# Transposes of x in pairs between the k and v matmuls of a transformer block on one core

## The chip, the core and the metric

The kernel runs on one core of a Trainium2 chip. The metric is the device time of one execution in microseconds (us). The core has five engines that run side by side, each working through its own instructions in order: PE does matmuls and transposes into PSUM banks, DVE, ACT and POOL work on tiles, SP issues the loads and stores. An instruction that needs another engine's result waits for a semaphore, and all that stands behind it on its own engine waits too.

## The reference

One layer of an encoder block, in float32, on x of 1024 rows and 1024 columns:

```
h = RMSNorm(x)
[q | k | v | u] = h @ w_in                 # widths 512, 128, 128, 512
a = GQA(q, k, v)                           # 8 query heads, 2 kv heads, axial RoPE, bidirectional
p = (windowed_mean(u) - u) @ pool_w + pool_b, times pool_scale   # 4 groups
x = x + concat([a, p]) @ w_out
x = x + SwiGLU(RMSNorm(x))                 # inner width 2816
```

## The kernel before

x lies in SBUF as eight tiles of 128 rows, `qp[:, t, :]`. PE needs it transposed, so for each of the eight column blocks k PE transposes the block of every row tile of a group (L474, one transpose of 128x128 for each tile) into one PSUM bank. The bank is emptied in two instructions: ACT multiplies by the norm's gain and writes the high part (L464), then DVE writes what is left of the value as the low part (L466). The full-precision product is made of three matmuls on high and low parts, and this holds for every product of the kernel.

`kv_tile(t)` projects row tile t to k and v. For each k it issues three matmuls of 128x256 (L490) into one bank, and at the end ACT (L498, L502) and DVE (L504) empty that bank. While a tile is projected, the next group of rows is transposed. `weave(tiles, ts)` mixes the two on PE: `tiles` are projected, and `turn_x(ts)` is advanced from time to time, one k at each step. The groups are rows 0, 1, 2 to 3 and 4 to 7, so there are three weaves with transposes: tile 0 projected while tile 1 is transposed (one transpose for each k), tile 1 while tiles 2 and 3 are (two), tiles 2 and 3 while tiles 4 to 7 are (four). Then tiles 4 to 7 are projected with no transposes between.

The banks: even k takes a bank of pool b1 (four banks, shared with the accumulators of `kv_tile`), odd k one of pool b2 (two banks). A transpose that takes a used bank waits until DVE's L466 has read it.

Around this stand the sums of squares of x (L451 on ACT) with a chain of tiny DVE instructions that make 1/rms of each row (L362 to L373), and the splitting of weights of w_in, loaded as 128x1024 pieces, into high and low parts: the high part on whichever engine the planner finds (L340 on ACT, L344 on POOL), the low part in `combine` (L355), on DVE or POOL. After the projections `spread_r` (L669) uses diagonal matrices of 1/rms, made 128 columns at a time on ACT (L656) and DVE (L658).

The order on PE follows the code. What other engines do is added as jobs to a planner (`flow`), which keeps an estimated time for each engine and a rank for each job, and writes each engine's instructions down in the order in which it lets them start; where an operation may run on two engines it takes the one that it holds to be free sooner. So what PE does earlier or later in the code changes the order on ACT, DVE and POOL too.

Of the kernel before, what the change touches and what calls it, by code (L numbers as in the profile page):

```python
# [289 lines left out]
def block_kernel(  # L290
# [167 lines left out]
    def turn_x(ts):  # L458
        n = len(ts) * P
        c0 = ts[0] * P  # L460

        def evacuate(hi, lo, pt, k):
            yield act(n, 0.05)
            nc.scalar.activation(hi, pt[:, :n], AF.Copy, scale=g1[:, k:k + 1])  # L464
            yield dve(n)
            nc.vector.scalar_tensor_tensor(lo, pt[:, :n], g1[:, k:k + 1], hi.bitcast(F32), op0=ALU.mult, op1=ALU.subtract)  # L466

        for k in range(NK):
            flow.now = max([flow.now] + [x_at[t, k] for t in ts])
            wide = k % K["wide"] == K["wide"] - 1  # L470
            pt = bank2()[:, 0:512] if wide else bank()
            flow.tensor(0.107 * len(ts))
            for i, t in enumerate(ts):
                nc.tensor.transpose(pt[:, i * P:(i + 1) * P], qp[:, t, k * P:(k + 1) * P], ident)  # L474
            job = flow.add(evacuate(hT(0, k, c0, n), hT(1, k, c0, n), pt, k))
            flow.hold("b2" if wide else "b1", job)
            for t in ts:
                x_turned[t, k] = job
            yield
# [4 lines left out]
    def kv_tile(t):  # L484
        pk = bank()
        for k in range(NK):
            hi, lo, job = wkv[k]
            flow.tensor(0.354, job, x_turned[t, k])
            for i, (a, b) in enumerate(PASSES):
                nc.tensor.matmul(pk[:, :2 * KW], hT(a, k, t * P, P), (hi, lo)[b], start=(k == 0 and i == 0), stop=(k == NK - 1 and i == 2))  # L490
            if k < NK - 1:
                yield

        def evacuate():
            r = rx[:, t:t + 1]
            yield [rx_job[t]]
            yield act(KW, 0.1)
            nc.scalar.activation(qp[:, t, AW:AW + KW], pk[:, 0:KW], AF.Copy, scale=r)  # L498
            pv = pk[:, KW:2 * KW].rearrange("p (h d) -> p h d", d=HD)
            hi, lo = vv[:, t, :, 0, :], vv[:, t, :, 1, :]  # L500
            yield act(KW, 0.1)
            nc.scalar.activation(hi, pv, AF.Copy, scale=r)  # L502
            yield dve(KW)
            nc.vector.scalar_tensor_tensor(lo, pv, r, hi.bitcast(F32), op0=ALU.mult, op1=ALU.subtract)  # L504

        kv_job[t] = flow.add(evacuate())
        flow.hold("b1", kv_job[t])
        yield
# [424 lines left out]
    def weave(tiles, ts=None):  # L933
        turns = turn_x(ts) if ts else None
        for i, b in enumerate([b for g in [kv_tile(t) for t in tiles] for b in [g] * NK]):
            next(b, None)
            if turns and i % len(tiles) == 0:
                next(turns, None)

    units = [(t, kv) for t in range(NT) for kv in range(NKV)]  # L940
# [589 lines left out]
    for i, ts in enumerate(groups):  # L1530
        for j in range(0, len(ts), 2):
            stats_x(ts[j:j + 2])
        for w, when in enumerate(K["take"]):
            if when == i:
                take_w(w)
        if i == K["tables"]:
            tab_job = load_tables()
        if i > 0 and ts[0] >= 4 and not kf:
            kf.append(flow.add(k_finish(0, 4)))
        weave(ts, groups[i + 1] if i + 1 < len(groups) else None)  # L1540
# [172 lines left out]
```

## Time and profile before

| | |
|---|---|
| median of 3 runs | 1082.85 us (1082.71 to 1082.98) |
| the profiled execution | 1083.04 us |
| its span in the trace | 1081.0 us |
| PE busy | 1061.1 us, 98% of the span |
| DVE busy | 742.1 us |
| ACT busy | 513.6 us |
| POOL busy | 459.0 us |

The span runs from the first to the last instruction in the trace; 2.04 us of the profiled execution's own time lie outside it, and that execution took 0.19 us more than the median. Busy shares are over the whole span: the stretch that the change touches ends some 32 us after its start.

### The profile page before, as it was taken

How to read it: one execution, taken by the hardware profiler on the slowest of the kernel's cores; microseconds unless marked ns; L12 is line 12 of the kernel's file. 1: busy time of each engine (PE TensorE's matmuls, PEld its weight loads, DVE VectorE, ACT ScalarE, POOL GpSimd, SP SyncE). 2: the span in 40 equal slices, each digit the busy share in tenths (PEclk: the TensorE clock that was granted, in tenths of full speed). 3: DMA queues.
4: the chain of work that ended last, by engine and by line, in shares of the span. 5: the costliest groups of instructions: out<-in, count | busy, mean ns of one | idle time of the engine just before them, and what ended most of it. 6: DMA issues, size and time to landing. Idle time of an engine off the chain costs nothing.

```text
span 1081.0 us, 13923 instructions
## 1 busy us (share of the span) xinstructions
PE 1061.1 (98%) x5114; PEld 876.2 (81%) x5114; DVE 742.1 (69%) x1210; ACT 513.6 (48%) x912; POOL 459.0 (42%) x371
## 2 busy tenths in 40 slices
PE   7999999999999999999999999999999999999998
PEld 6887877878888888878878887888788878888787
DVE  7888678788776766784984479355954496448845
ACT  6614478666666654633343433434433443343340
POOL 3153444444223223463643555345534464445431
PEclk9999999999999999999999999999999999999999
DMA  7212110000000100221023102220212013110114
GB/s 260 69 40 79 39 59 30 10 21 10 20 21 11 30 21 30 59 98 39 19 68 109 39 1 78 78 79 1 78 59 76 23 33 104 59 40 20 40 58 156
DMA packets 42707, 58.47 MB, mean 54 GB/s; under 512 B 4240, under 2 KB 32784, under 8 KB 42640
## 3 DMA queue, kind: packets, MB, share of 16 engines
q1 hardware_dynamic: 42640, 57.59, 16.9%
q8 instruction: 40, 0.66, 0.2%
q14 instruction: 27, 0.22, 0.1%
HBM read 53.39 MB, written 4.19 MB: 53 GB/s over the span
## 4 chain that ended last, share of the span: by engine, by line
PE 79%; DVE 10%; issue 3%; POOL 3%; ACT 3%; DMA 1%; SPq 0%; POOLq 0%; ACTq 0%; DVEq 0%
PE b L1180 36%; PE b L912 8%; PE b L1498 8%; PE b L875 5%; PE b L832 5%; PE b L862 4%; PE b L688 4%; PE b L601 3%; DVE wk L355 3%; POOL wk L355 2%; PE b L1445 2%; DVE qp L1460 2%; PE b L490 2%; DVE ring L355 1%; DVE nm L841 1%
## 5 line engine op out<-in xcount | busy, mean ns | idle before, releaser
L1180 PE MATMUL b<-wk,ring 128*128 128x512 f32 x1872 | 426.8, 389 | 1.2 <-POOL ring L355 0.9
L1180 PEld LDWEIGHTS b<-wk,ring 128*128 128x128 f32 x1872 | 351.0, 188 | 75.6 <-POOL ring L355 1.8
L340 ACT ACTIVATE ring<-raw 128x512 fp32r<-128x512 f32 x130 | 81.5, 629 | 121.2 <-PE b L1180 59.9
L851 POOL TENSOR_SCALAR wk<-wk,rsm 128x1024 f32<-128x1024 f32 x64 | 75.0, 1180 | 132.9 <-PE b L862 40.7
L349 DVE TENSOR_TENSOR wk<-b,wk 128x512 fp32r<-128x512 f32 (+1 forms) x160 | 102.0, 659 | 42.5 <-ACT wk L340 42.1
L340 ACT ACTIVATE wk<-b 128x512 fp32r<-128x512 f32 (+1 forms) x160 | 90.4, 577 | 82.6 <-PE b L862 65.6
L355 POOL TENSOR_TENSOR ring<-raw,ring 128x512 fp32r<-128x512 f32 x49 | 63.3, 1292 | 149.5 <-ACT ring L340 136.0
L1498 PE MATMUL b<-raw,ring 128*128 128x512 f32 x480 | 113.4, 393 | 1.1 <-DVE qp L1460 1.1
L355 DVE TENSOR_TENSOR ring<-raw,ring 128x512 fp32r<-128x512 f32 x81 | 63.7, 789 | 72.2 <-ACT ring L340 71.7
L1498 PEld LDWEIGHTS b<-raw,ring 128*128 128x128 f32 x480 | 88.6, 188 | 24.3 <-DVE qp L1460 3.8
L1460 DVE TENSOR_TENSOR qp<-qp,b 128x512 f32<-128x512 f32 (+1 forms) x157 | 100.5, 673 | 9.0 <-PE b L1445 8.9
L912 PE MATMUL b<-wk 128*128 128x512 f32 x384 | 102.5, 397 | 0.0
L355 POOL TENSOR_TENSOR wk<-wk 128x512 fp32r<-128x512 f32 (+3 forms) x51 | 71.5, 1409 | 43.5 <-ACT wk L340 20.3
L832 PE MATMUL b<-kT,wk 128*128 128x512 f32 x256 | 89.4, 431 | 0.3 <-ACT wk L808 0.3
L875 PE MATMUL b<-wk,vv 128*128 128x512 f32 x256 | 82.7, 399 | 3.9 <-DVE wk L349 3.9
L841 DVE TENSOR_REDUCE nm<-b 128x1 f32<-128x1024 f32 x64 | 78.0, 1219 | 11.3 <-PE b L832 10.2
L1498 PE MATMUL b<-wk,ring 128*128 128x512 f32 x360 | 83.3, 389 | 0.0
L912 PEld LDWEIGHTS b<-wk 128*128 128x128 f32 x384 | 70.7, 188 | 14.9
L1498 PEld LDWEIGHTS b<-wk,ring 128*128 128x128 f32 x360 | 67.5, 188 | 14.2
L862 PEld LDWEIGHTS b<-ident,wk 128*128 128x128 f32 x512 | 63.6, 140 | 16.5
L862 PE MATMUL b<-ident,wk 128*128 128x128 f32 x512 | 76.4, 272 | 0.0
L843 ACT ACTIVATE wk<-b,nm 128x1024 f32<-128x1024 f32 x64 | 71.4, 1116 | 10.4 <-DVE nm L841 9.5
(144 smaller groups left out, 1445.1 us busy)
## 6 DMA issues: line engine op xcount, KB each, us to landing
raw<-in_w_gate_dram SPq DMA_DIRECT2D x22, 512.0 KB, 3.7
raw<-in_w_up_dram SPq DMA_DIRECT2D x22, 512.0 KB, 3.9
wk<-in_w_down_dram SPq DMA_DIRECT2D x20, 512.0 KB, 4.7
raw<-in_w_in_dram SPq DMA_DIRECT2D x10, 512.0 KB, 3.8
raw<-in_w_out_dram SPq DMA_DIRECT2D x8, 512.0 KB, 3.5
out_dram<-qp SPq DMA_DIRECT2D x15, 256.0 KB, 2.0
qp<-in_x_dram SPq DMA_DIRECT2D x7, 512.0 KB, 9.7
raw<-in_x_dram SPq DMA_DIRECT2D x14, 256.0 KB, 2.8
```

The source lines that it names most:

```text
L340: nc.scalar.activation(hi, src, AF.Copy)
L349: nc.vector.tensor_tensor(lo, src, hi.bitcast(F32), op=ALU.subtract)
L355: (nc.gpsimd if way[0] == "G" else nc.vector).tensor_tensor(dst, a, b, op=op)
L832: nc.tensor.matmul(s[:, c * 512:(c + 1) * 512], qT[t][0][:, h * P:(h + 1) * P], kT[:, kv, b, c * 512:(c + 1) * 512], start=(b == 0), stop= ...
L841: nc.vector.tensor_reduce(nm, s, axis=AX, op=ALU.max, negate=True)
L851: nc.gpsimd.tensor_scalar(pe, pe, rs, 1.0, op0=ALU.mult, op1=ALU.mult)
L862: nc.tensor.transpose(pt[:, j * P:(j + 1) * P], pe[:, c * P:(c + 1) * P], ident)
L875: nc.tensor.matmul(po[t, kv], vt, ps[:, b], start=(c == 0 and b == 0), stop=(c == NT - 1 and b == 1))
L912: nc.tensor.matmul(self.py, mix[self.t][a][:, k, :], wo[k][b][:, self.cs], start=(self.i == 0 and i == 0), stop=(self.i == NK - 1 and i == 2))
L1180: nc.tensor.matmul(bank_, w[0][:, a, i], x[:, b], start=(start and i == 0 and j == 0), stop=(stop and i == PARTS - 1 and j == 2), skip_gro ...
L1460: nc.vector.tensor_tensor(dst, dst, src, op=op)
L1498: nc.tensor.matmul(banks[t][0], x[:, a, t * P:(t + 1) * P], y[:, b], start=(own == name and i == 0 and j == 0), stop=(i == 1 and j == 2), ...
```

## The change

In `weave`, transposes are issued for one k after every k-step of the tiles together. Now they are issued for two k after every second such step:

```diff
         for i, b in enumerate([b for g in [kv_tile(t) for t in tiles] for b in [g] * NK]):
             next(b, None)
-            if turns and i % len(tiles) == 0:
+            if turns and i % (2 * len(tiles)) == 0:
+                next(turns, None)
                 next(turns, None)
```

On PE, in the third weave (tiles 2 and 3 projected, four transposes for each k), this is the order before from the first matmuls of tile 2 on. Numbers such as `b_356` name one bank tile; `b_349` and `b_415` are the accumulators of tiles 2 and 3.

```order
L490 MATMUL b_349<-wk 128x256 x3
L474 MATMUL b_356<-ident,qp 128x128 x4
L490 MATMUL b_349<-wk 128x256 x6
L474 MATMUL b_371<-ident,qp 128x128 x4
L490 MATMUL b_349<-wk 128x256 x6
L474 MATMUL b_392<-ident,qp 128x128 x4
L490 MATMUL b_349<-wk 128x256 x6
L474 MATMUL b_405<-ident,qp 128x128 x4
L490 MATMUL b_349<-wk 128x256 x3
L490 MATMUL b_415<-wk 128x256 x3
L474 MATMUL b_427<-ident,qp 128x128 x4
L490 MATMUL b_415<-wk 128x256 x6
```

And the same stretch with the change; accumulators are now `b_347` and `b_414`, and the transposes' banks in turn of k are `b_353`, `b_359`, `b_389`, `b_396`, `b_426`, `b_432`, `b_456`, `b_462`.

```order
L490 MATMUL b_347<-wk 128x256 x3
L474 MATMUL b_353<-ident,qp 128x128 x4
L474 MATMUL b_359<-ident,qp 128x128 x4
L490 MATMUL b_347<-wk 128x256 x12
L474 MATMUL b_389<-ident,qp 128x128 x4
L474 MATMUL b_396<-ident,qp 128x128 x4
L490 MATMUL b_347<-wk 128x256 x9
L490 MATMUL b_414<-wk 128x256 x3
L474 MATMUL b_426<-ident,qp 128x128 x4
L474 MATMUL b_432<-ident,qp 128x128 x4
L490 MATMUL b_414<-wk 128x256 x12
L474 MATMUL b_456<-ident,qp 128x128 x4
```

The transposes of every odd k have moved ahead of six matmuls (in the two weaves before, of three); the sixth of the eight, `b_442` before and `b_432` now, has 15 matmuls of its weave behind it before and 21 now.

On DVE, in the same weave, before (`b1` and `b2` are the pools of the banks, `raw` a loaded weight, L355 a weight's low part, L362 to L373 the chain for 1/rms):

```order
L466 SCALAR_TENSOR_TENSOR wk_116<-b2_340,pk_72,wk_108 128x256
L466 SCALAR_TENSOR_TENSOR wk_117<-b1_356,pk_72,wk_109 128x512
L355 TENSOR_TENSOR wk_175<-raw_172,wk_174 128x1024
L504 SCALAR_TENSOR_TENSOR vv_94<-b1_261,rx_121,vv_94 128x2x64
L362 TENSOR_SCALAR ms_387<-ssq1_122 128x2
L466 SCALAR_TENSOR_TENSOR wk_117<-b2_371,pk_72,wk_109 128x512
L364 TENSOR_SCALAR ra_388<-ms_387 128x2
L466 SCALAR_TENSOR_TENSOR wk_118<-b1_392,pk_72,wk_110 128x512
```

And with the change:

```order
L466 SCALAR_TENSOR_TENSOR wk_117<-b1_353,pk_72,wk_109 128x512
L371 SCALAR_TENSOR_TENSOR ra_274<-ra_274,ms_273 128x1
L355 TENSOR_TENSOR wk_175<-raw_172,wk_174 128x1024
L373 SCALAR_TENSOR_TENSOR rx_121<-ra_274,rx_121 128x1
L466 SCALAR_TENSOR_TENSOR wk_118<-b1_389,pk_72,wk_110 128x512
L362 TENSOR_SCALAR ms_384<-ssq1_122 128x2
L466 SCALAR_TENSOR_TENSOR wk_117<-b2_359,pk_72,wk_109 128x512
L504 SCALAR_TENSOR_TENSOR vv_94<-b1_261,rx_121,vv_94 128x2x64
L364 TENSOR_SCALAR ra_385<-ms_384 128x2
```

The 128x1024 weight split L355 still follows the first emptying (L466 of `b_353`), but two instructions of the 1/rms chain now lie around it; the emptyings of the second and third k have changed places, and with the emptying of tile 1's accumulator (L504 of `b_261`) they stand behind the split.

On ACT, at the end of the projections, before (`b_569` and `b_608` are the accumulators of tiles 6 and 7, L673 empties the first bank of `spread_r`):

```order
L656 ACTIVATE wk_651<-ident_73,rx_121 128x128 x4
L498 ACTIVATE qp_84<-b1_569,rx_121 128x128
L502 ACTIVATE vv_94<-b1_569,rx_121 128x2x64
L656 ACTIVATE wk_651<-ident_73,rx_121 128x128 x4
L498 ACTIVATE qp_84<-b1_608,rx_121 128x128
L673 ACTIVATE wk_672<-b1_673 128x512
```

And with the change (tile 7's accumulator is `b_611`):

```order
L498 ACTIVATE qp_84<-b1_569,rx_121 128x128
L656 ACTIVATE wk_655<-ident_73,rx_121 128x128 x4
L502 ACTIVATE vv_94<-b1_569,rx_121 128x2x64
L498 ACTIVATE qp_84<-b1_611,rx_121 128x128
L502 ACTIVATE vv_94<-b1_611,rx_121 128x2x64
L656 ACTIVATE wk_655<-ident_73,rx_121 128x128 x4
```

The second four diagonals now stand behind both instructions that empty tile 7's bank, and on DVE L658 for them stands behind that tile's L504. Beyond this stretch SP's order is the same in every row and the matmuls of the feed-forward part are too, except for the pool that some banks come from; of the weight splits with 128x1024 elements two that DVE did (one in the attention, the load of w_out) are done by POOL.

## Rows read from the trace of the kernel before

**Rows 1.** The page: busy time of each engine.

```profile
PE 1061.1 (98%) x5114; PEld 876.2 (81%) x5114; DVE 742.1 (69%) x1210; ACT 513.6 (48%) x912; POOL 459.0 (42%) x371
```

**Rows 2.** Windows; stretch, length, busy PE, PEld, DVE, ACT, POOL; granted clock, DMA share, GB/s.

```profile
10.66:15.50 4.84, 4.84 (x23) 4.84 (x24) 4.19 (x18) 1.90 (x6) 1.98 (x3) 1.00 1.03 420
15.50:31.80 16.30, 14.84 (x125) 14.28 (x125) 15.24 (x48) 12.78 (x28) 5.57 (x4) 1.00 0.61 176
...
200.00:1060.00 860.00, 856.48 (x4030) 705.40 (x4029) 572.59 (x844) 401.51 (x704) 379.56 (x291) 1.00 0.15 45
```

**Rows 3.** PE's waits by line and releaser: us in total, times, longest.

```profile
PE b L474 <- DMA qp<-in_x_dram: 5.0, 2, 4.3
PE b L875 <- DVE wk L349: 3.9, 7, 1.4
...
PE b L474 <- DVE wk L466: 1.5, 2, 1.3
...
PE b L601 <- POOL wk L355: 0.9, 1, 0.9
```

**Rows 4.** The chain of waits on PE: start, duration, what.

```profile
12.63 0.21 PE b L474
12.85 0.64 PE b L490 x3
...
15.96 0.12 PE b L474
...
30.46 0.44 PE b L474 x4
30.90 0.71 PE b L490 x6
...
32.05 11.88 PE b L490 x99
```

**Rows 5.** PE's timeline: start, duration, instruction, idle before it and the releaser.

```profile
19.37 0.41 PE L474 MATMUL b<-ident,qp 128*128 128x128 f32 x2 [0.18 <-DVE ra L369]
...
21.70 0.60 PE L474 MATMUL b<-ident,qp 128*128 128x128 f32 x4
...
29.09 0.66 PE L474 MATMUL b<-ident,qp 128*128 128x128 f32 x4 [1.28 <-DVE wk L466]
...
43.77 1.55 PE L688 MATMUL b<-wk 128*128 128x512 f32 x6
45.15 1.07 PE L669 MATMUL b<-wk 128*128 128x512 f32 x4
```

**Rows 6.** DVE's timeline in the third weave.

```profile
24.12 2.00 DVE L355 TENSOR_TENSOR wk<-raw,wk 128x1024 fp32r<-128x1024 f32 x1
26.05 0.34 DVE L504 SCALAR_TENSOR_TENSOR vv<-b,rx,vv 128x128 fp32r<-128x128 f32 x1
26.31 2.07 DVE L362 TENSOR_SCALAR ms<-ssq 128x2 f32<-128x2 f32 x1
28.30 0.74 DVE L466 SCALAR_TENSOR_TENSOR wk<-b,pk,wk 128x512 fp32r<-128x512 f32 x1
28.95 0.15 DVE L364 TENSOR_SCALAR ra<-ms 128x2 int32<-128x2 int32 x1
```

**Rows 7.** POOL's timeline in the third weave.

```profile
24.01 1.05 POOL L344 TENSOR_SCALAR wk<-raw 128x1024 fp32r<-128x1024 f32 x1 [3.26 <-DMA raw<-in_w_in_dram]
25.14 3.21 POOL L355 TENSOR_TENSOR wk<-raw,wk 128x1024 fp32r<-128x1024 f32 x1
```

**Rows 8.** ACT's timeline in the third weave: sum of squares, then one emptying.

```profile
23.30 1.06 ACT L451 ACTIVATE wk<-qp 128x1024 f32<-128x1024 f32 x1
...
24.59 0.70 ACT L464 ACTIVATE wk<-b,pk 128x512 fp32r<-128x512 f32 x1
```

**Rows 9.** Timeline of ACT and DVE before `spread_r`.

```profile
42.88 0.38 ACT L502 ACTIVATE vv<-b,rx 128x128 fp32r<-128x128 f32 x1
43.13 1.29 ACT L656 ACTIVATE wk<-ident,rx 128x128 fp32r<-128x128 f32 x4
...
43.63 1.18 DVE L658 SCALAR_TENSOR_TENSOR wk<-ident,rx,wk 128x128 fp32r<-128x128 f32 x4
```

**Rows 10.** Timeline in the attention: PE's waits and the DVE split ahead of the first.

```profile
157.55 1.23 DVE L355 TENSOR_TENSOR wk<-raw,wk 128x1024 fp32r<-128x1024 f32 x1
...
160.57 0.50 PE L875 MATMUL b<-wk,vv 128*128 128x512 f32 x1 [0.60 <-DVE wk L349]
...
180.49 0.50 PE L875 MATMUL b<-wk,vv 128*128 128x512 f32 x1 [1.35 <-DVE wk L349]
```

## The prediction

> **What bounds the kernel now.** I began with the page: PE is busy for 1061.1 of 1081.0 us, every other engine for less than 70% [rows 1]. An edit that leaves PE's work as it is can therefore move the time in two ways only: by PE's idle time, and by the pace of its matmuls. The windows say where idle time is left [rows 2]: 1.46 us in the stretch that ends at 31.80, which holds the second and third weave, and 3.5 us in the 860 us from 200 us on. PE's waits name the releasers [rows 3]: the loads of x (5.0 us) and, for the transposes, DVE's L466 (1.5 us in two waits). The rest belongs to later stages: 3.9 us in seven waits of the attention's L875, 0.9 us of L601.
>
> For the pace I took the chain of waits, which lists a piece's length without overlap [rows 4]. At 12.6 us a transpose and three matmuls take 0.21 + 0.64 us. Later three matmuls take half of 0.71, or 0.36, and 99 in one run take 11.88, or 0.120 each. The granted clock reads 1.00 in each window [rows 2], but the two paces (0.213 and 0.120 for the same matmul) stand nearly as the levels of 1.2 and 2.4 GHz do; the slow one ends with a transpose of 0.12 us at 15.96. The Trainium skill (TensorE: Matmul & The Clock Gate, HAM oscillation — how this bites in real kernels) says that waits between groups of matmuls bring the lower level back; this trace shows a PE that starts slow and never falls back.
>
> **What the edit removes and adds.** The number of transposes and matmuls is the same. If going from transposes to matmuls and back cost something, half of these turns would be saved. The rows show no such cost: four transposes and six matmuls take 0.44 + 0.71 = 1.15 us, and six matmuls in the long run without transposes 0.72 [rows 4]. So 0 for the saved turns.
>
> First and second weave: odd k come three matmuls sooner, so their banks must be empty 0.36 us sooner (0.64 at the slow pace). PE has one wait there, 0.18 us at 19.37 [rows 5]; it may go, or come back at another pair. I take 0, with 0.3 either way. The first weave lies before 15.5 us, so it also leaves the slow stretch as it is.
>
> Third weave: PE reaches the transposes of `b_353` at the 21.70 us at which it reached `b_356` [rows 5], since the work ahead is equal. If nothing held it, two pairs and twelve matmuls each would follow: `b_426`, the fifth k, would stand at 21.70 + 2 x (0.87 + 1.45) = 26.3 us (four transposes 0.435, twelve matmuls 1.45).
>
> Its bank is the one that L466 of `b_389` empties, and that stands on DVE behind L371, the split L355 and L373. Step by step. ACT came to `b_356` at 24.59 [rows 8] behind two sums of squares (1.06 each) and one L498; now a sum and the L498 come later, so `b_353` is read from about 23.0 to 23.7 (an L464 takes 0.70) and L466 (0.74 [rows 6]) ends at about 24.4. POOL's L344 has begun at 24.01 and lasts to 25.06 [rows 7]. In the trace of before DVE's L355 beside it took 2.00, and ended 1.06 after POOL was done; POOL's own L355 from 25.14 took 3.21 but ended 2.23 after DVE's [rows 6, 7]. The two behave as if one must wait for the other, so their bare lengths are 1.06 and 2.23, and L362, with two columns only, took 2.07 instead of the 0.15 of its like while POOL's ran [rows 6]. With the change L371 reaches DVE inside POOL's L344 and waits to 25.06; then the two L355 follow each other in either order to about 28.4, and L373, whichever comes first, ends at 28.6. L466 of `b_389` then ends at 29.35, where before it was L466 of `b_371` that let PE go on at 29.09.
>
> So `b_426` waits for about 3 us, from 26.3 to 29.4. `b_432` needs L466 of `b_359`, next on DVE with L362 before it: 30.1. After this sixth group of transposes 21 matmuls of the weave are left, where 15 were left at 29.09. The end of the weave moves by 30.13 - 29.09 + 6 x 0.12 = **+1.8 us**. All later banks come in time: `b_456` waits for nothing before 31.9. Should `b_426` have to wait for tile 1's accumulator instead, whose L504 (0.34 [rows 6]) follows, then it starts at 30.45, `b_432` at 30.9, and the term is +2.55. The lower end is a rival below.
>
> The Trainium skill (SBUF — State Buffer, "Who interferes with whom") has it that a DVE instruction with two SBUF inputs and a POOL instruction reading SBUF exclude each other, and that whichever issues first holds the port to its end. The 2.00 and 3.21 agree, but 2.07 of L362, which has one SBUF input, goes beyond the two-input case.
>
> `spread_r`: L669 comes 1.38 us after L688's first six begin (43.77 and 45.15), and its four matmuls follow at some 0.23 (1.07 in all, the modelled ends overlap), so the second half needs its high part at 45.6 and its low part at 45.85 [rows 5]. Its second four diagonals stood ahead of tile 7's emptying and now stand behind L498 and L502 (0.25 each, as L656 follows L502 at 42.88 and 43.13 [rows 9]), which wait for tile 7's last matmul, at about 43.8 where L688 begins. ACT does them (1.29 for four) from 44.5 to 45.8, and DVE's L658 ends about 0.4 later, at 46.2, where before it ended 0.39 after L656 too (44.81 and 44.42 [rows 9]). The need at 45.85 is missed by **+0.4 us** (0 if ACT gets through the emptying without delay, 0.8 if it waits for more).
>
> The rest: SP's order is unchanged. The weight split at 157.55 (1.23 us) goes from DVE to POOL, shortly before a wait of PE for DVE of 0.60 at 160.57; another is 1.35 at 180.49 [rows 10]. With other places on POOL it may as well cost what it gives. I take 0; bounds -1.95 and about as much above.
>
> Sum: 1.8 + 0.4 = 2.2 us. On the profiled execution's 1083.04 (span 1081.0 and 2.04 outside) this is 1085.24; that execution was 0.19 above the median, so **1085.1 us**. A measurement of this kernel tells 0.2% from no change, that is 2.17 us: up to 1085.02 counts as the same. My forecast lies on this bound.
>
> **The rivals.** *The port goes the other way (not slower).* The whole stall hangs on L466 of `b_353` being done at 24.4, after POOL's L344 started at 24.01 [rows 7]. If ACT is 0.4 us sooner, or the load that L344 waited 3.26 us for comes 0.4 later, L371 and DVE's L355 go first and are done by about 25.1; POOL then waits, not DVE. Then L466 of `b_389` waits for its transposes only and ends near 26.4, `b_432` waits to 27.4, some 0.8 us for PE instead of 1.46. Total -0.66 + 0.4 on the median: about 1082.6. For it: the margin is small. Against: ACT's work ahead of `b_353` must shrink by more than I see. Chance 0.12. With the attention's two waits gone as well (1.95 us, below) it would be 1080.6, faster by 0.2%: 0.06, counted apart.
>
> *The clock falls back.* The longest stop of PE after 16 us is 1.35 us at 180.49, and none was followed by slow matmuls; mine is 3 us. At the start PE went slow from 10.66 to about 15.41, 4.75 us, in which a step took 0.85 instead of 0.48 [rows 4]: 2.1 us lost. If the stop brings this again, the sum is 4.3 and the time 1087.2. Chance 0.20. By the skill's sentence on pauses this is what would happen; no run here shows at what length of a stop.
>
> *The attention gives it back.* PE's order there is the same, so what is lost by 46 us stays lost, unless DVE, with a split less, ends the 0.60 wait, or that and the 1.35: 1084.4 to 1083.1, say 1084.0. Chance 0.18.
>
> *The forecast itself*, 0.44. Its own range, from 0.3 less in the first weaves and no `spread_r` term to the other bank: 1084.3 to 1085.9.
>
> **How the numbers follow.** Slower by over 0.2%: the part of the forecast above 1085.02 (0.28) and the clock (0.20), 0.48. Within 0.2%: the rest of the forecast (0.16), the give-back (0.18), the port (0.12), 0.46. Faster: 0.06. From 1082.6 to 1087.6 the range takes in the clock's case with some variation and the port's, and leaves out the faster case and the outer part of those two.
>
> **What would show it.** In the third weave PE should wait for DVE's L466 before L474 at about 26.3, for 3 us, and again for 0.3 us; DVE's L371 or L355 should begin beside POOL's L344 and L373 end near 28.6. Matmuls after the stop at 0.12 us each speak against the clock, at 0.21 for it. L669 should wait about 0.4 us for DVE's L658 or not at all. Windows from 200 us on should give PE the same busy time. If the third weave's waits come to under 1.5 us the prediction fails in the order of the port; if the time moves while the weave's end stays, it fails in the attention.

## The result: slower, 1091.54 us

The change takes 1091.54 us (1090.03 to 1092.3, 4 runs) beside 1082.78 us for the kernel before in the same session: ratio 1.0082, 95% interval 1.007 to 1.0094. The profiled execution of the change took 1092.3 us, with a span of 1090.2; that is 9.2 us more than the span before.

The page of the change [as rows 1]: PE is busy 5.0 us longer with the same 5114 matmuls. So only part of the loss is idle time; the rest lies in matmuls whose rows are longer, by a lower clock in the third weave (the windows below) and, in the down projections, by waits for weights, which the page counts as busy (further below).

```profile
PE 1066.1 (98%) x5114; PEld 877.5 (80%) x5114; DVE 741.0 (68%) x1211; ACT 513.0 (47%) x912; POOL 463.3 (42%) x370
```

Windows of the change [as rows 2]. The granted clock of the third weave's stretch is no longer 1.00; a window laid on the slow part alone, from 30.1 to 33.5 us, shows 0.50, which is the lower level of 1.2 GHz.

```profile
15.50:31.80 16.30, 13.55 (x104) 12.88 (x103) 14.75 (x43) 11.65 (x26) 5.63 (x5) 0.95 0.63 181
...
16.50:29.38 12.88, 10.21 (x88) 9.77 (x86) 11.37 (x31) 10.32 (x24) 5.63 (x4) 1.00 0.58 160
30.10:33.50 3.40, 3.40 (x16) 3.40 (x17) 3.30 (x12) 1.34 (x2) 0.00 (x0) 0.50 0.49 142
33.55:47.02 13.47, 13.47 (x115) 13.47 (x114) 10.50 (x47) 9.90 (x25) 0.00 (x0) 1.00 0.15 41
```

PE's waits [as rows 3]: the transposes wait 2.57 us for DVE's L466 at one place. A wait is there that the kernel before does not have, five times, for DVE and a tile named raw at L1499 (line 1498 of the kernel before, the matmuls of the down projections).

```profile
PE b L875 <- DVE wk L349: 4.2, 8, 1.6
PE b L474 <- DVE wk L466: 2.8, 2, 2.6
PE b L1499 <- DVE raw L355: 2.5, 5, 0.5
...
PE b L601 <- POOL wk L355: 0.3, 1, 0.3
```

PE's timeline in the third weave [as rows 5]. The eight transposes that follow the stop take 1.84 us where eight took 1.04 before it, and the first L688 starts at 47.02 instead of 43.77.

```profile
24.35 1.04 PE L474 MATMUL b<-ident,qp 128*128 128x128 f32 x8
25.14 1.67 PE L490 MATMUL b<-wk 128*128 128x256 f32 x12
29.38 1.84 PE L474 MATMUL b<-ident,qp 128*128 128x128 f32 x8 [2.57 <-DVE wk L466]
30.87 2.85 PE L490 MATMUL b<-wk 128*128 128x256 f32 x12
...
47.02 1.55 PE L688 MATMUL b<-wk 128*128 128x512 f32 x6
48.41 1.60 PE L669 MATMUL b<-wk 128*128 128x512 f32 x4
```

DVE and POOL in the same stretch [as rows 6, 7]: L371, L355 and L373 one behind the other, and L373, one column wide, takes 2.30 us while POOL's L355 runs.

```profile
23.80 0.75 DVE L466 SCALAR_TENSOR_TENSOR wk<-b,pk,wk 128x512 fp32r<-128x512 f32 x1 [0.19 <-ACT wk L464]
24.47 0.83 DVE L371 SCALAR_TENSOR_TENSOR ra<-ra,ms 128x1 f32<-128x1 f32 x1
25.23 1.21 DVE L355 TENSOR_TENSOR wk<-raw,wk 128x1024 fp32r<-128x1024 f32 x1
26.36 2.30 DVE L373 SCALAR_TENSOR_TENSOR rx<-ra,rx 128x1 f32<-128x1 f32 x1
28.58 0.74 DVE L466 SCALAR_TENSOR_TENSOR wk<-b,pk,wk 128x512 fp32r<-128x512 f32 x1
29.24 0.15 DVE L362 TENSOR_SCALAR ms<-ssq 128x2 f32<-128x2 f32 x1
29.31 0.74 DVE L466 SCALAR_TENSOR_TENSOR wk<-b,pk,wk 128x512 fp32r<-128x512 f32 x1
```

```profile
24.25 1.05 POOL L344 TENSOR_SCALAR wk<-raw 128x1024 fp32r<-128x1024 f32 x1 [3.39 <-DMA raw<-in_w_in_dram]
25.38 3.26 POOL L355 TENSOR_TENSOR wk<-raw,wk 128x1024 fp32r<-128x1024 f32 x1
```

To see where the rest of the 9.2 us lies, I subtracted the start of the n-th matmul in the trace of before from that of the n-th in the trace of the change. The difference is 0.5 us at 18 us, 3.3 at the end of the projections, 3.9 behind `spread_r`, 3.3 from 105 us on (the wait of L601 is 0.6 shorter), 4.1 for a while in the attention and 3.3 again, 2.4 at 487 us, where the feed-forward part begins, and then it rises by some 1.34 us in each of the five down projections, to 9.1. So two thirds of the loss lie 500 us behind the last instruction that the diff touches. The first of the five, in the trace of the change: PE's weight loads, its matmuls, and then DVE.

```profile
540.27 0.19 PEld L1499 LDWEIGHTS b<-wk,ring 128*128 128x128 f32 x1 [0.20 <-POOL wk L355]
540.82 2.14 PEld L1499 LDWEIGHTS b<-wk,ring 128*128 128x128 f32 x10 [0.36 <-DVE ring L355]
```

```profile
543.23 2.65 PE L1499 MATMUL b<-raw,ring 128*128 128x512 f32 x9
546.11 1.20 PE L1499 MATMUL b<-raw,ring 128*128 128x512 f32 x4 [0.23 <-DVE qp L1461]
547.82 2.56 PE L1499 MATMUL b<-raw,ring 128*128 128x512 f32 x10 [0.50 <-DVE raw L355]
```

```profile
539.22 1.55 DVE L355 TENSOR_TENSOR ring<-wk,ring 128x512 fp32r<-128x512 f32 x1
...
545.98 1.18 DVE L355 TENSOR_TENSOR ring<-silu,ring 128x512 fp32r<-128x512 f32 x1
547.08 0.68 DVE L355 TENSOR_TENSOR raw<-wk,raw 128x512 fp32r<-128x512 f32 x1
```

And PE and DVE at the same place of the kernel before, where the last 13 matmuls run without a stop for raw:

```profile
542.92 3.44 PE L1498 MATMUL b<-raw,ring 128*128 128x512 f32 x13 [0.22 <-DVE qp L1460]
...
542.97 1.00 DVE L355 TENSOR_TENSOR raw<-wk,raw 128x512 fp32r<-128x512 f32 x1
543.89 0.68 DVE L355 TENSOR_TENSOR ring<-silu,ring 128x512 fp32r<-128x512 f32 x1
```

The last two low parts have changed places: PE waits for the raw one, and with the change it is made second. By the starts of the matmuls this stop is 0.60 of the 1.34 us. Another 0.38 go at 541 us, where the weight loads wait for low parts of POOL and DVE (the PEld lines; DVE's took 1.55 us), and 0.36 at 545 us, where a weight load waits 0.52 us for DVE's L1461. In each down projection DVE also makes six such raw parts where it made four, and POOL two where it made four (30 and 10 in all, 20 and 20 before).

The program says how a change in the first 32 us can do that. The kernel plans itself six times. Each rehearsal gives every job a rank (how soon its result is needed), the next rehearsal uses those ranks, and the kernel is built with the ranks of the rehearsal that the planner's own sums hold to be the fastest:

```
    for _ in range(K["rehearsals"]):
        flow = block_kernel(Nothing(), *[Nothing() for _ in args], ranks)
        best = min(best, (flow.now, ranks), key=lambda b: b[0])
        ranks = flow.needs()
```

Before, the second rehearsal is chosen; with the change, the fifth, and by the planner's own sums the plan of the change is the faster of the two. So the kernels differ in a second way that stands in no line of the diff: the ranks of all 1325 jobs. My theory from here on: the down projections pay for the ranks, and the third weave for the pairs, DVE's collision with POOL and the clock. The rival: the pairs cost it everywhere, by what they bring the planner or the chip into the later stages.

### The profile page after: what moved, and what is told of

It is laid out like the page before. It is cut to its first block, busy times and chain, and to the rows that moved or that the text cites. A ratio compares the mean times of both kernels' runs of the same rounds, so it can differ in the third digit from the quotient of the medians.

```text
span 1090.2 us, 13914 instructions
## 1 busy us (share of the span) xinstructions
PE 1066.1 (98%) x5114; PEld 877.5 (80%) x5114; DVE 741.0 (68%) x1211; ACT 513.0 (47%) x912; POOL 463.3 (42%) x370
## 4 chain that ended last, share of the span: by engine, by line
PE 78%; DVE 12%; issue 4%; POOL 3%; ACT 2%; DMA 1%; SPq 0%; ACTq 0%; POOLq 0%; DVEq 0%
PE b L1181 35%; PE b L912 8%; PE b L1499 8%; PE b L875 5%; PE b L832 5%; PE b L862 5%; PE b L688 3%; PE b L601 3%; DVE wk L355 3%; DVE ring L355 2%; PE b L1446 2%; PE b L490 2%; POOL wk L355 2%; DVE qp L1461 2%; DVE nm L841 1%
## 5 line engine op out<-in xcount | busy, mean ns | idle before, releaser
L355 POOL TENSOR_TENSOR ring<-raw,ring 128x512 fp32r<-128x512 f32 x54 | 70.0, 1297 | 157.8 <-ACT ring L340 138.8
L1499 PE MATMUL b<-raw,ring 128*128 128x512 f32 x480 | 115.2, 394 | 4.1 <-DVE raw L355 2.5
L1499 PEld LDWEIGHTS b<-raw,ring 128*128 128x128 f32 x480 | 88.6, 188 | 29.1 <-DVE qp L1461 5.9
L355 DVE TENSOR_TENSOR ring<-raw,ring 128x512 fp32r<-128x512 f32 x76 | 57.8, 762 | 77.2 <-ACT ring L340 77.2
L1461 DVE TENSOR_TENSOR qp<-qp,b 128x512 f32<-128x512 f32 (+1 forms) x157 | 102.0, 677 | 9.0 <-PE b L1446 8.9
L1499 PE MATMUL b<-wk,ring 128*128 128x512 f32 x360 | 85.0, 392 | 0.2
L355 POOL TENSOR_TENSOR wk<-wk 128x512 f32<-128x512 f32 (+3 forms) x49 | 70.4, 1445 | 32.2 <-ACT wk L340 23.1
L355 POOL TENSOR_TENSOR ring<-silu,ring 128x512 fp32r<-128x512 f32 x35 | 54.0, 1543 | 63.3 <-ACT ring L340 63.3
L1499 PEld LDWEIGHTS b<-wk,ring 128*128 128x128 f32 x360 | 67.2, 188 | 16.4 <-DVE ring L355 1.8
```

The source lines that it names most:

```text
L355: (nc.gpsimd if way[0] == "G" else nc.vector).tensor_tensor(dst, a, b, op=op)
L1461: nc.vector.tensor_tensor(dst, dst, src, op=op)
L1499: nc.tensor.matmul(banks[t][0], x[:, a, t * P:(t + 1) * P], y[:, b], start=(own == name and i == 0 and j == 0), stop=(i == 1 and j == 2), ...
```

## The experiments

Most of them separate the order of the transposes from the ranks. `PER` is the number of k turned at a time (1 as before, 2 as in the change); ranks can then be rehearsed with one and the kernel built with the other. The diffs below give the sense of each edit in short, not its exact lines.

**Pairs with the ranks of before, and the reverse.**

```diff
+    PER[0] = 1
     for _ in range(K["rehearsals"]):
...
+    PER[0] = 2
     with tile.TileContext(nc) as tc:
         block_kernel(tc, *args, best[1])
```

> The pairs of the change, but planned with the ranks that the planner had chosen for the kernel before (its second rehearsal instead of the fifth); PE's order is that of the change, and from the pool mixer on every engine's order is that of before. If the 5 to 6 us after the projections come from the other ranks: 1085 to 1087 us (third weave's stall of about 2 us, with or without 1.7 us of slow clock), and the five waits of PE for DVE in the down projections are gone. If the pairs themselves cost them: 1091 us and the five waits stay.

> The other way round: transposes one by one as before, planned with the ranks that the planner chose for the change. If the ranks are the cause: PE's third weave ends at 43.8 to 44.5 us, but five waits of 0.5 us in the down projections, 1.34 us lost at each, 1088 to 1089 us in all. If the pairs are: 1083 us.

Measured: pairs with old ranks 1087.76 us, 1.0052 (1.0037 to 1.0067); singles with new ranks 1092.17 us, 1.0091 (1.0076 to 1.0106). With the old ranks no down projection loses anything. With the new ones, and no pair in the kernel, all five waits are there, and the starts drift by 1.34 to 1.38 us at each. PE's waits in the run with singles:

```profile
PE b L474 <- DVE wk L466: 2.7, 4, 1.5
PE b L1498 <- DVE raw L355: 2.5, 5, 0.5
...
PE b L764 <- POOL wk L355: 1.9, 1, 1.9
...
PE b L601 <- POOL wk L355: 1.1, 1, 1.1
```

So the theory holds for the down projections. For the third weave, take the time from the 61st to the 181st matmul of the program (from inside the second weave to the projections behind the third): 16.06 us before, 16.95 with pairs and old ranks, 16.16 with singles and new ranks. It goes with the pairs. The loss at `spread_r` goes with the ranks: the starts drift there by 0.0 us with pairs and old ranks and by 0.8 with singles and new ranks.

Both totals came out higher than I expected, 0.8 us over the upper figure with old ranks and 3.2 with new ones. In both, POOL's low parts for the weights of the pool mixer and of q are late near 100 us (its L355 stands there behind high parts of ACT). The same ranks do not give the same order once the transposes come differently: with pairs and old ranks the order on DVE, ACT and POOL is that of before only from some 99 us on, not from the pool mixer on as the expectation says. That the lateness comes from ranks used with an order for which they were not rehearsed is my reading. No run isolates it, and the last run below, which has no pairs and at this place the change's ranks too, does not have it. The run with pairs and old ranks shows what it costs, a stop at 99 to 102 us and behind it matmuls at the lower clock:

```profile
99.38 0.50 PE L601 MATMUL b<-wk 128*128 128x512 f32 x1 [0.58 <-ACT wk L340]
101.81 5.06 PE L601 MATMUL b<-wk 128*128 128x512 f32 x14 [1.93 <-POOL wk L355]
```

```profile
103.15:106.50 3.35, 3.35 (x10) 2.57 (x9) 1.82 (x2) 1.29 (x2) 0.04 (x1) 0.50 0.71 282
```

**PE's stop filled with needless matmuls.** Their results are not used.

```diff
             next(b, None)
+            if len(ts or ()) == 4 and i == 8:
+                for _ in range(20):
+                    nc.tensor.matmul(last["b2"][:, 512:768], hT(0, 0, 2 * P, P), wkv[0][0], start=True, stop=True)
```

> The change with 20 needless matmuls of 128x256 (2.4 us) on PE ahead of the transposes that wait in the third weave, into the unused half of a bank tile. If PE's stop is what lowers its clock: granted clock 1.00 throughout, the first 128x512 matmuls of the pool mixer's projection at about 45.3 us instead of 47.0, 1089.8 us. If the slow stretch has another cause: it stays at 30 to 33.5 us, 1091.5 us.

Measured: 1090.07 us, 1.0075 (1.0059 to 1.0092), 1.5 us under the change's median (0.8 by the two ratios to the kernel before), with a granted clock of 1.00 in the third weave and in all four runs. The needless matmuls are L936. The wait ahead of the transposes is 0.40 us, and the eight transposes and twelve matmuls behind it take 1.38 and 1.68 where they took 1.84 and 2.85. The first L688 starts at 44.47, 0.8 us sooner than expected; the 61st matmul, in the second weave, already starts 1.2 us sooner than in the profile of the change, since PE left its slow start earlier in this execution. The total agrees with the one execution of the change whose mean granted clock was 1.000: 1090.03 us.

```profile
25.39 2.56 PE L936 MATMUL b<-wk 128*128 128x256 f32 x20
28.36 1.38 PE L474 MATMUL b<-ident,qp 128*128 128x128 f32 x8 [0.40 <-DVE wk L466]
29.49 1.68 PE L490 MATMUL b<-wk 128*128 128x256 f32 x12
```

With the stop unfilled, a mean clock of 1.000 was kept by 9 of 24 executions (1 of 4 of the change, and 4 of 10 in each of two runs below, whose order is the same up to 524 us at least); with the stop filled by 4 of 4, and with the stop removed, below, by 10 of 10. So the stop is what lets the clock fall, though not every time.

**Pairs in the first two weaves alone**, ranks of before.

```diff
-            if turns and i % len(tiles) == 0:
-                next(turns, None)
+            per = 2 if len(tiles) < 2 else 1
+            if turns and i % (per * len(tiles)) == 0:
+                [next(turns, None) for _ in range(per)]
```

> Pairs in the first two weaves alone, ranks of before. By the prediction's step the first two weaves cost 0 with 0.3 either way: 1082.5 to 1083.1 us, third weave as before. If pairs cost wherever they stand, by stops or turned orders: over 1083.5 us.

Measured: 1088.89 us, 1.0061 (1.0046 to 1.0076), a miss by 6 us. It is not the weaves: the first L688 starts at 43.98 us, 0.2 later than before. What costs it is low parts of POOL that are late as above: two stops for POOL near 100 us (1.4 and 2.6 us), of which the longer is

```profile
106.97 2.50 PE L764 MATMUL b<-wk 128*128 128x512 f32 x5 [2.58 <-POOL wk L355]
```

and the clock behind them: two executions with a mean granted clock of 1.000 took 1087.4 and 1087.9, two with 0.997 took 1089.9 and 1090.0.

**The change with the ranks of before from the second feed-forward block on.** Up to there every engine's order is that of the change.

```diff
+    ranks = ranks_of_the_change[:583] + ranks_of_before[583:]
     with tile.TileContext(nc) as tc:
-        block_kernel(tc, *args, best[1])
+        block_kernel(tc, *args, ranks)
```

> The change with the ranks of its own plan up to the first block of the steady feed-forward part, and from there on (job 583 of 1325) the ranks chosen for the kernel before. If the five times 1.34 us come from the order that the ranks give there: the waits for DVE's raw tile are gone, 1091.5 - 6.7 = 1084.8 us, or 1083 in an execution without the slow clock. If they come from the state that the planner or the chip brings into that part: 1091 us.

Measured: 1084.65 us, 1.0017 (1.0007 to 1.0027). The five waits are gone and the down projections drift by nothing. Ten executions fall into two groups by their mean granted clock: four with 1.000 have a median of 1083.3, six with 0.998 one of 1084.95.

**Ranks of before in the last four down projections only**, 78 jobs each; all others keep those of the change.

> The change with its own ranks, except for the jobs of the last four of the five down projections (78 jobs each), which keep the ranks of before. If the order inside the down projections is what costs 1.34 us each: four of five losses go, 1091.5 - 5.4 = 1086.1 us, one wait of 0.5 us for DVE's raw tile is left. If the loss is brought in by the blocks ahead of them: 1091 us.

Measured: 1085.56 us, 1.0024 (1.0014 to 1.0033). One wait of 0.5 us is left, and the starts drift by 1.38 us at the first down projection and by nothing at the other four. The order inside them is what costs; the blocks ahead with the change's ranks cost nothing. Which part of it costs how much, the raw part made second, the ten parts moved to DVE or the other late low parts, was not tried apart.

**POOL taken out of the third weave.** POOL's L344 and L355 there split the second weight of the pool mixer, which is first needed behind the projections. The planner meant them for later, but POOL has nothing ahead of them and starts when the load lands. With the high part made on ACT, which gets to it behind the weave, POOL has to wait for ACT. Base: the run with ranks of before in the feed-forward part.

```diff
-        way = flow.quicker(act(n), dve_copy(n), pool_scale(n)) if both and not ffn else act(n)
+        way = flow.quicker(act(n), dve_copy(n), pool_scale(n)) if both and not ffn and not flow.force else act(n)
...
-                take_w(w)
+                flow.force = w == 1; take_w(w); flow.force = 0
```

> The run pair_ffn_old with one edit more: the high part of the second pool weight is made on ACT behind the third weave, not on POOL at 24 us, so that POOL's L355 no longer runs beside DVE in that weave. If that collision is the stall: DVE's L373 takes 0.15 instead of 2.3 us, PE's waits in the third weave come to 0.5 us, the first L688 starts at 43.8 us instead of 47.0 and the clock stays up, 1081.5 us if the pool mixer's stage keeps its time. If the pairs stall by the bank alone: a wait of over 2 us stays.

> The kernel before, no pairs, with that same edit of the second pool weight. If the collision with POOL is also what PE waits for before the change: the waits of 1.46 us in the third weave go, the first L688 starts at 42.3 us, 1080.7 us if the pool mixer's stage keeps its time. Rival: another emptying is late then, 1082.2 us.

Measured with pairs: 1080.78 us, 0.9985 (0.9975 to 0.9994), ten of ten executions at a clock of 1.000. L373 takes 0.15 us, the transposes of the third weave wait no longer for L466, and the first L688 starts at 42.65, sooner than expected because no wait at all is left. Through the third weave the order on PE, ACT and DVE is that of the base run, so POOL alone makes the difference there. Its L355 in this run, and DVE:

```profile
37.30 2.41 POOL L355 TENSOR_TENSOR wk<-raw,wk 128x1024 fp32r<-128x1024 f32 x1 [16.45 <-ACT wk L340]
```

```profile
24.46 0.15 DVE L371 SCALAR_TENSOR_TENSOR ra<-ra,ms 128x1 f32<-128x1 f32 x1
24.53 1.22 DVE L355 TENSOR_TENSOR wk<-raw,wk 128x1024 fp32r<-128x1024 f32 x1
25.66 0.15 DVE L373 SCALAR_TENSOR_TENSOR rx<-ra,rx 128x1 f32<-128x1 f32 x1
25.73 0.74 DVE L466 SCALAR_TENSOR_TENSOR wk<-b,pk,wk 128x512 fp32r<-128x512 f32 x1
```

```profile
42.65 1.55 PE L688 MATMUL b<-wk 128*128 128x512 f32 x6
```

Without pairs: 1083.42 us, 1.0007 (0.9998 to 1.0016). The third weave's waits are gone there as well and the first L688 starts at 41.52, but the pool mixer's stage gives back 1.0 us by 105 us and 1.2 by 145, with new waits of L764 (0.8) and L804 (1.4) for POOL; the expectation holds for the weave and fails for the total.

**The change's ranks for the turn to the feed-forward part alone**, no pairs.

> The kernel before, no pairs, with the change's ranks for the jobs 479 to 583 alone (the turn to the feed-forward part). The change won 0.9 us there; if its ranks did that, 1081.3 us. If it was the state that it came with, 1082.2 us.

Measured: 1081.32 us, 0.999 (0.9981 to 1.0), 1.1 us under the kernel before. The starts fall back by 0.89 us near 487 us, as in the change. So the new ranks win 0.9 us there, and lose 6.7 later.

**No pairs, with all that helped.** The 59 jobs of the first part have the ranks of before, the jobs up to 583 those of the change, the rest those of before, and the second pool weight goes to ACT.

> No pairs, the second pool weight's high part on ACT, and the ranks as in pair_act_split but for the 59 jobs of the first part (those of before). It tells what pairing itself is worth once POOL is out of the third weave. If turns between transposes and matmuls cost nothing: third weave without waits, as fast from 18 us to its end as pair_act_split within 0.2 us, and 1080.8 us if the pool mixer's stage comes out alike. If pairs win by fewer turns (8 saved): the weave 0.3 us or more slower.

Measured: 1080.89 us, 0.9983 (0.9974 to 0.9992). From the 61st to the 181st matmul PE takes 14.35 us in each of the three runs without POOL in the third weave, with pairs or without, and took 16.06 in the profile of before. Pairing is worth nothing and costs nothing once the emptyings are in time.

## Why the prediction was wrong

The time lies 4 us over the range. The step that failed is *the rest*: "I take 0; bounds -1.95 and about as much above." It rested on SP's order, on PE's order in the feed-forward part and on two weight splits, all of which held. What it did not look at was DVE's and POOL's order inside the down projections, whose splits are of 128x512 (I had compared those of 128x1024). There the changed choice among the rehearsals put a low part that PE waits for behind another, made others late and moved ten from POOL to DVE: 1.34 us at each of five, 6.7 us in all. The ranks of before give them back, and four of five come back where only the last four have them. The sign that I had named, the same busy time of PE from 200 us on, failed there: 39.84 us in the first down projection instead of 39.15. No rival had this: mine let the later stages differ by one split only. The unforeseen gains of the same ranks are smaller, 0.6 us at L601 and 0.9 at the turn to the feed-forward part. So the rest came to +5.2 us, where I had 0 and at most some 1.95.

The other steps, with the term of the forecast first:

- *Turns between transposes and matmuls, 0:* right, 14.35 us with pairs and without.
- *The third weave, +1.8:* right in its mechanism and nearly in its rows. L373's end was put at 28.6 and is 28.66; the two L466 were put at 29.35 and 30.1 and end at 29.32 and 30.05. The sixth transposes start at 30.10 (below), 1.0 us behind 29.09, and six matmuls are 0.72: 1.7 us. It varies with the landing of the load that starts POOL: where L344 began at 23.36 instead of 24.25 (ranks of before in the feed-forward part), the weave ended 0.9 us later than before. In both, the transposes go on 5.1 to 5.2 us after L344 began; I had reckoned 5.3 from a start at 24.01, so the agreement within 0.1 us is in part luck. Taking POOL away removed all of it. The chain of waits of the change, behind the stop:

```profile
30.10 1.12 PE b L474 x4
31.22 2.50 PE b L490 x12
```

- *The clock falls back, a rival of 0.20 priced at 2.1 us:* it came, by the mean clock of 0.998, in three of four executions of the change. The price is 1.65 us by the two groups of ten executions (1084.95 - 1083.3), and 1.7 by the window: 3.4 us at half the clock.
- *`spread_r`, +0.4:* L669's four matmuls take 1.60 instead of 1.07, +0.5, and the starts behind drift by 0.59. The late diagonals come with the new ranks, not with the pairs: with old ranks the four take 1.07.
- *The port goes the other way, 0.12:* it did not; L371 came to DVE at 24.47, after POOL's L344 at 24.25. The rule of the Trainium skill (SBUF — State Buffer, "Who interferes with whom"), that a DVE instruction with two inputs in SBUF and a POOL instruction that reads SBUF block each other and the first to issue goes first, agrees with this trace: L371 and L373 have two such inputs, L371 (0.83 us) ends at 25.30 with POOL's L344, and L373 (2.30) at 28.66 beside the end of POOL's L355 at 28.64.

In sum for the change's profile: third weave with clock and start 3.3, `spread_r` 0.6, L601 -0.6, turn -0.9, down projections 6.7, which is 9.1 of 9.2 us. That 1084.65 us with the old feed-forward ranks is within 0.5 us of my 1085.1 is in part chance: 1.5 us of terms that I had, 1.7 us of clock in six executions of ten, less the 1.5 us of gains that I had not.

## What to carry to other kernels

Where a planner writes the order, a two-line edit can choose another plan for the whole kernel: compare every engine's order to the end of the program, above all on the engines that PE waits for, and time the edit once with the old plan's ranks before saying what the edit does. The planner's own sums do not tell it: here they held the slower plan to be the faster. An engine with nothing queued ahead of a job starts it when its data land, whatever the plan meant; if that job shares something with a busy engine, put a step of it behind that stage on an engine that is in order. A stop of PE like the one of 2.57 us here has to be priced twice, once as idle time and once, with a chance, as slow matmuls behind it.

## What the runs showed of the hardware that was not expected

A one-column instruction on DVE (L373) took 2.30 us beside a POOL instruction of 128x1024, fifteen times the 0.15 us that it takes with POOL out of the stretch.

After a PE stop of 2.2 to 2.6 us in the third weave the granted clock fell to 0.50 in some executions and not in others of the same kernel (by the mean clock, three of four and twice six of ten). It did not fall in the profile of before after its stop of 1.28 us, nor in that of singles with new ranks after one of 1.54; with the long stop filled or removed it stayed at 1.00 in 4 of 4 and 10 of 10. The end of the slow start also moves from one execution to the next: the 61st matmul starts between 17.9 and 19.5 us, though the work ahead of it is nearly the same in all these kernels.
